# Hybrid decoder step on one core: the recurrence's input tiles moved one tile ahead of its gate tiles, and three steps of the sample attention moved by one or two half steps

## The chip, the cores and the metric

The kernel runs on one core of one Trainium2 chip. The metric is the device time of the whole program in microseconds (us). Engines are called as in the profile: PE is TensorE's matmul pipeline, PEld its weight loads, DVE VectorE, ACT ScalarE, POOL GpSimd, SP the engine that issues the DMAs. L1302 is line 1302 of the kernel. Lines from L105 on stand two or three higher in the changed kernel.

## The reference, cut to what matters

One layer of a decoder for a prompt of 512 tokens and a sample group of 8 x 8 tokens, which share the weights. One input projection feeds a sparse attention with three branches (compressed, selected, window) and a gated linear recurrence; both are merged and projected out.

```
z = einsum('btd,dc->btc', rms(x), w_in)       # one projection, 9776 columns
q, kv, g_nsa, g_att, x_rnn, g_rnn, gm_att, gm_rnn = split(z)
# recurrence, 1024 channels
xc = conv_b + sum(x_ext[:, k:k+T] * conv_w[k] for k in range(4))
r  = sigmoid(blockdiag(xc, w_rg) + b_rg)
i  = sigmoid(blockdiag(xc, w_ig) + b_ig)
log_a = -8 * r * softplus(-lru_lambda)
a, u  = exp(log_a), sqrt(-expm1(2*log_a)) * (i * xc)
h_t   = a_t * h_(t-1) + u_t
u_rnn = (h * silu(g_rnn)) @ w_rnn_out
# sample attention
o_cmp = softmax(q k_c) v_c                    # 64 compressed blocks
idx   = top_k(importance, 15)                 # from o_cmp's probabilities
o_sel = softmax(q k[idx], q k_new) v          # gathered blocks
o_win = softmax(q k_window) v_window          # last 512 tokens
```

## The kernel before, in words

All work is written out by hand in one order; every engine runs its own instructions strictly in that order and waits on semaphores. All weights are split into a high and a low part (`whi`, ACT, L233; `wlo`, DVE, L239), so that a product is three matmuls (L1798 to L1800). The projection is done in column tiles of 128; a tile is four **slots**, each with 24 of these matmuls of 288 columns. The main loop over slots emits, in this order: the high split of weights due, the sample attention's next half step if it is due, the low split, the evacuation of the sums of the slot before, the functions put behind this slot (`at(slot, fn, True)`), and then the slot's 24 matmuls.

`column_tiles()` sets the order of the tiles. The recurrence's channels come as eight chunks `c` of 128: tile `("rx", c)` holds its input, tile `("rg", c)` its gate path.

The sample's attention starts with these tiles. It runs over four **pairs** of sequences, one pair every six steps; a step is two **half steps** (0 and 1) and `put(t, half, order, f, x)` places a function. Half steps are spread evenly over the slots, so some slots have none. In half 0 stand `s_turn` (PE transposes of the exponentials into the two `t` banks, copied out by ACT as `spt`), `s_out` (values into banks `o` and `m`) and `k_scores` (into the two `s` banks, read by `k_max` on DVE and `s_exp` on ACT). A pair begins with `x_scores` (compressed scores, half 0, both `s` banks), read by `x_exp` (maximum on DVE, exponential on ACT, two additions on DVE); `x_sum` (one transposing product into a `t` bank, half 1 of the next step) feeds `x_select` on DVE, the choice of blocks. A pair ends with `x_turn_` (six transposes, both `t` banks), `x_turned` (five ACT copies to `vx`), `x_out` (products with `vx`), `s_sum` (DVE reads banks `o` and `m`), `s_fin` and `s_put`.

A chunk of the recurrence is a chain. When its `rx` tile is evacuated, `rnn_chunk(c, xr)` puts the convolution's first part on ACT (`xc`) and DVE; the rest of the convolution stands one slot later, `split` (high and low part of `xc`: `xb`, and of the block-diagonal weights: `bdh`, `bdl`) two slots later. From the third slot on `gate_0` is ready to be emitted, then `gate_1`: each is four matmuls (L1302) into one `s` and one `t` bank, and four ACT tanh that read them (`tr`, `ti`, L1305). A gate step is emitted only in a slot whose half step has none of `x_scores`, `k_scores`, `s_turn`, `x_turn_`, `c_norm`:

```
if gates and not taken:
    behind.setdefault(s, []).append(gates.pop(0))
```

One slot after `gate_1` follows `decay` (ACT exponential, tanh, square root; two DVE products), two slots after it `scan` (DVE; then two small ACT copies `hout`). `rnn_gated` multiplies by the gate path once both are there.

Slots are counted below from the one in which chunk 0's `rx` tile is evacuated (slot 0). In the trace of before, slot 4 begins near 736.2 us, slot 7 at 748.7, slot 13 at 778.9, slot 17 at 797.8, slot 28 at 859.4, slot 35 near 891.4.

Of the kernel before, what the change touches and what calls it, by code (L numbers as in the profile page):

```python
# [84 lines left out]
def column_tiles():  # L85

    off = dict(q=0, kv=1024, gn=2560, ga=2608, rx=3632, rg=4656, gma=5680, gmr=7728)

    def kv(br, s, g):
        return off["kv"] + ((br * 2 + s) * KG + g) * HD + np.arange(HD)  # L90

    tiles = [(("gn",), off["gn"] + np.arange(48))]
    fill = [(("ga", j), off["ga"] + j * 128 + np.arange(128)) for j in range(8)]
    fill += [(("gm", 1, j), off["gmr"] + j * 128 + np.arange(128)) for j in range(16)]
    fill += [(("gm", 0, j), off["gma"] + j * 128 + np.arange(128)) for j in range(16)]
    for g in range(KG):
        if g:
            tiles += [fill.pop(0) for _ in range(3)]
        tiles.append((("c", g), np.concatenate([kv(0, 0, g), kv(0, 1, g)])))
        tiles.append((("v", g), np.concatenate([kv(1, 1, g), kv(2, 1, g)])))  # L100
        tiles.append((("k", g), np.concatenate([kv(1, 0, g), kv(2, 0, g)])))
        for rp in range(2):
            tiles.append((("q", g, rp), off["q"] + (g * 4 + rp * 2) * HD + np.arange(128)))
    left = len(fill) - (EARLY - 9)
    tiles += fill[:-left]  # L105
    for c in range(8):
        tiles.append((("rx", c), off["rx"] + c * 128 + np.arange(128)))
        tiles.append((("rg", c), off["rg"] + c * 128 + np.arange(128)))
    tiles += fill[-left:]
    return tiles  # L110

# [2 lines left out]
def nsa_rglru_step(ctx, tc, a, o):  # L114
# [54 lines left out]
    tiles = []  # L169
# [21 lines left out]
    for n, (kind, m, units) in enumerate(tiles):  # L191
# [19 lines left out]
        for u in range(len(units)):  # L211
            late = len(units) == 1 or u == 0 and tiles[n - 1][0][0] == "G"
            at = base - 2 if late else base - 3 if u == 0 else base - 1
# [109 lines left out]
    for c in range(8):  # L323
        for b in range(2):
            k = 2 * c + b
            x = xs[c][:, b]
# [41 lines left out]
    def at(slot, fn, last=False):  # L368

        (behind if last else later).setdefault(slot, []).append(fn)  # L370

    now = [0]
# [302 lines left out]
    for g in range(KG):  # L675
        for i in range(4):
            for br in range(3):
                x = Group()
# [473 lines left out]
    def sample_steps():  # L1152

        steps = {}

        def put(t, half, order, f, *args):
            steps.setdefault(2 * t + half, []).append((order, len(steps.get(2 * t + half, [])), f, args))

        for x in pairs:
            s = 2 + 6 * x.n
            if x.b[0].b >= KEPT:
                for y in x.b:
                    put(s - 5, 1, 0, c_fetch, y)
            put(s - 2, 0, 9, q_pair, x)
            e = s - 3 if x.n else s - 2
            put(e, 0, 0, c_square, x)
            put(e, 1, 5, c_norm, x)
            put(e, 1, 7, c_root, x)  # L1170
            put(e + 1, 1, 7, c_keys, x)
            put(s, 0, 4, x_scores, x)
            put(s, 0, 8, x_exp, x)
            put(s, 1, 7, x_prob, x)
            put(s, 1, 9, x_new, x)
            put(s + 1, 1, 5, x_sum, x)
            put(s + 1, 1, 6, x_select, x)
            for k, n2 in enumerate((4, 0, 1, 2, 3)):
                t = s + 1 + k
                put(t - 1, 0, 0, k_load, x, n2)  # L1180
                put(t, 1, 0, v_load, x, n2)
                put(t, 0, 4, k_scores, x, n2)
                put(t, 0, 8, k_max, x, n2)
                put(t, 0, 9, s_exp, x, n2)
                put(t + 1, 0, 1, s_turn, x, n2)
                put(t + 1, 0, 1.5, s_turned, x, n2)
                put(t + 2, 0, 2, s_out, x, n2)
            put(s + 5, 1, 9, s_factors, x)
            put(s + 6, 1, 7, s_total, x)
            put(s + 6, 1, 1, x_turn_, x)  # L1190
            put(s + 6, 1, 1.5, x_turned, x)
            put(s + 7, 0, 4.5, x_out, x)
            put(s + 7, 1, 8, s_sum, x)
            put(s + 8, 1, 5, s_fin, x)
            put(s + 8, 1, 8, s_put, x)
        for t in range(max(steps) + 1):
            fs = [f for _, _, f, _ in steps.get(t, [])]
            taken.extend(f for f in fs if f in (x_scores, k_scores, s_turn, x_turn_, c_norm))
            for _, _, f, args in sorted(steps.get(t, []), key=lambda e: e[:2]):
                f(*args)  # L1200
            yield (t + 1) / (max(steps) + 1)
# [8 lines left out]
    gates, taken = [], []  # L1210

    def load_bd(c):
        t = rp_["p"].tile([128, 2, 128], F, tag="bd", name="bd", bufs=2)
        S.dma_start(t, a["w_bd"][c])
        bd[c] = t
# [42 lines left out]
    def rnn_chunk(c, xr):  # L1258
        p = rp_["p"]

        def rt(name):
            return p.tile([128, NT], F, tag="rt", name=name, bufs=5)

        if c + 1 < 8:
            load_bd(c + 1)
        xc = rt("xc")
        xs_ = xr[:, 515:603].rearrange("p (b s) -> p b s", s=11)
        V.tensor_copy(cvout[:, c, 0, :], xr[:, 512:515])
        V.tensor_copy(cvout[:, c, 1:, :], xs_[:, :, 8:11])
        xcs = xc[:, SEQ:].rearrange("p (b t) -> p b t", t=8)  # L1270
        A.activation(xc[:, :SEQ], xr[:, 0:SEQ], AF.Identity, bias=P("cb", c), scale=P("cw", c * 4))
        A.activation(xcs, xs_[:, :, 0:8], AF.Identity, bias=P("cb", c), scale=P("cw", c * 4))

        def tap(k):
            w = P("cw", c * 4 + k)
            V.scalar_tensor_tensor(xc[:, :SEQ], xr[:, k:k + SEQ], w, xc[:, :SEQ], OP.mult, OP.add)
            V.scalar_tensor_tensor(xcs, xs_[:, :, k:k + 8], w, xcs, OP.mult, OP.add)

        tap(1)
        at(now[0] + 1, lambda: (tap(2), tap(3)), True)  # L1280
        tr, ti, aa = rt("tr"), rt("ti"), rt("aa")

        xb = []

        def split():

            split_bd(c)
            for w in range(2):
                me, other = slice(w * 64, w * 64 + 64), slice(64 - w * 64, 128 - w * 64)
                t = p.tile([128, NT], R, tag=f"xb{w}", name="xb", bufs=1)  # L1290
                A.activation(t[me], xc[me], AF.Copy)
                V.tensor_sub(t[other], xc[me], t[me].bitcast(F))
                xb.append(t)

        def gate(w):

            me = slice(w * 64, w * 64 + 64)
            for h in range(2):
                hs = slice(h * HF, h * HF + HF)
                b = bank("st"[h])  # L1300
                for k in range(2):
                    T.matmul(b[:, :HF], bd[c][k][:, w, :], xb[w][:, hs], start=k == 0, stop=k == 1)  # L1302
                for n, t in enumerate((tr, ti)):
                    z = slice(n * 64, n * 64 + 64)
                    A.activation(t[me, hs], b[z, :HF], AF.Tanh, scale=0.5, bias=lc[z, 2 + w, c:c + 1])  # L1305

        def decay():
            A.activation(aa, tr, AF.Exp, scale=lc[:, 0, c:c + 1], bias=lc[:, 0, c:c + 1])
            A.activation(tr, tr, AF.Tanh, scale=lc[:, 1, c:c + 1], bias=lc[:, 1, c:c + 1])
            A.activation(tr, tr, AF.Sqrt, scale=0.25)  # L1310
            V.scalar_tensor_tensor(ti, ti, 1.0, xc, OP.add, OP.mult)
            V.scalar_tensor_tensor(ti, aa, 1.0, ti, OP.add, OP.mult)

        def scan():
            V.tensor_mul(ti, ti, tr)
            u0, a0 = ti[:, SEQ::8], aa[:, SEQ::8]
            V.tensor_mul(xc[:, 0:8], a0, sth[:, c])
            V.tensor_add(u0, u0, xc[:, 0:8])
            V.memset(a0, 0.0)
            hh = p.tile([128, NT], F, tag="hh", name="hh", bufs=1)  # L1320
            V.tensor_tensor_scan(hh, aa, ti, 0.0, OP.mult, OP.add)
            A.activation(hout[:, c, 0:1], hh[:, SEQ - 1:SEQ], AF.Copy)
            A.activation(hout[:, c, 1:], hh[:, SEQ + 7::8], AF.Copy)
            held["hh", c] = hh
            if ("s", c) in held:
                rnn_gated(c)

        at(now[0] + 2, split, True)

        def gate_0():  # L1330
            gate(0)
            gates.append(gate_1)

        def gate_1():
            gate(1)
            at(now[0] + 1, decay, True)
            at(now[0] + 2, scan, True)

        at(now[0] + 3, lambda: gates.append(gate_0))

    def rnn_gated(c):

# [310 lines left out]
    for s, (n, h, u) in enumerate(slots):  # L1653
# [98 lines left out]
        for n2 in range(n, len(tiles)):  # L1752
            if slot_of[n2] > s + 3:
                break
            name, j = tiles[n2][0][0], tiles[n2][0][-1]
            if name in ("ua", "ur") and s >= slot_of[last_g + 1] and (name == "ur", j) not in gates_in:
                t = gates_in[name == "ur", j] = rp_["p"].tile([128, NT], F, tag="tgi", name="tgi", bufs=4)
# [25 lines left out]
        for step, (h2, k) in enumerate([(h, k) for k in range(8)]):  # L1783
            kk = u * 8 + k
            name = kind[0]
# [115 lines left out]
```

## Time and profile before

| | |
|---|---|
| Time, median of 3 runs | 1646.51 us (1645.73 to 1646.8) |
| The profiled execution's own time | 1646.57 us |
| Its span, first to last instruction | 1644.5 us |
| PE busy | 1603.1 us, 97% of the span |
| DVE, ACT, POOL busy | 67%, 47%, 19% of the span |
| Mean granted TensorE clock | 0.992 of full speed |

Busy time of PE counts pipelined matmuls, so it says where PE stood still, not how fast it was while busy. The clock column says that: 1.0 is 2.4 GHz, 0.5 is 1.2 GHz.

### The profile page before, as it was taken

What the parts mean: (1) busy time and instruction counts of PE and PEld (TensorE: products, weight loads), DVE (VectorE), ACT (ScalarE), POOL (GpSimd) and SP (SyncE); (2) the same over time, 40 slices, a digit from 0 to 9 for tenths busy, and PEclk for the clock granted to TensorE, in tenths of its full rate; (3) what the DMA queues carried; (4) which work ended last, traced back from release to release, by engine and by line L of the source; (5) the groups of instructions that cost most, each with busy time, mean ns of one, the idle gap of its engine ahead of it and who ended that gap; (6) DMA issues with size and microseconds to landing.
All of it is one profiled execution on the core that took longest, in us unless ns stands there. A gap on an engine that the chain in (4) does not pass through costs nothing.

```text
span 1644.5 us, 34197 instructions
## 1 busy us (share of the span) xinstructions
PE 1603.1 (97%) x13293; PEld 1550.9 (94%) x13293; DVE 1104.0 (67%) x2159; ACT 775.9 (47%) x1429; POOL 305.7 (19%) x361
## 2 busy tenths in 40 slices
PE   9999999999999999999898999999999999999999
PEld 8989989998999999998788889999999999999999
DVE  7768778766876786666566575766666433458785
ACT  6353545454445554448666677444444222234332
POOL 0014443533443345400000000000000111110000
PEclk9999999999999999999999999999999999999999
DMA  6178534433443344448575674633328444466431
GB/s 231 63 273 273 187 106 130 161 114 107 157 140 112 116 147 157 146 140 256 180 227 192 218 236 142 202 140 126 126 107 300 157 163 147 143 219 218 150 136 70
DMA packets 131956, 271.91 MB, mean 165 GB/s; under 512 B 19793, under 2 KB 59858, under 8 KB 131538
## 3 DMA queue, kind: packets, MB, share of 16 engines
q1 hardware_dynamic: 131794, 269.73, 49.0%
q8 instruction: 104, 1.70, 0.4%
q14 instruction: 58, 0.48, 0.1%
HBM read 235.04 MB, written 43.02 MB: 169 GB/s over the span
## 4 chain that ended last, share of the span: by engine, by line
PE 47%; ACT 3%; DVE 3%; issue 0%; DMA 0%; POOL 0%; SPq 0%; ACTq 0%
PE g L1798 9%; PE g L1799 9%; PE g L1800 9%; PE g L1448 2%; PE g L1447 2%; PE g L1446 2%; PE g L1548 2%; PE g L1547 2%; PE g L1546 2%; PE t L1448 1%; PE t L1446 1%; PE t L1447 1%; PE s L941 1%; PE s L1548 1%; PE s L1546 1%; PE s L1547 1%
## 5 line engine op out<-in xcount | busy, mean ns | idle before, releaser
L1798 PE MATMUL g<-xh,whi 128*128 128x288 f32 x1920 | 580.8, 303 | 0.1
L1800 PE MATMUL g<-xh,wlo 128*128 128x288 f32 x1920 | 569.8, 297 | 3.7 <-DVE wlo L239 3.7
L1799 PE MATMUL g<-xl,whi 128*128 128x288 f32 x1920 | 570.1, 297 | 0.1
L1798 PEld LDWEIGHTS g<-xh,whi 128*128 128x128 f32 x1920 | 364.8, 190 | 17.0 <-issue 14.4
L1800 PEld LDWEIGHTS g<-xh,wlo 128*128 128x128 f32 x1920 | 364.2, 190 | 4.2 <-DVE wlo L239 4.2
L1799 PEld LDWEIGHTS g<-xl,whi 128*128 128x128 f32 x1920 | 364.7, 190 | 1.7 <-DVE xl L321 0.3
L239 DVE TENSOR_TENSOR wlo<-raw,whi 128x1024 fp32r<-128x1024 f32 x164 | 215.7, 1315 | 73.8 <-ACT whi L233 73.2
L879 POOL TENSOR_TENSOR cr<-cr,wcs 128x512 f32<-128x512 f32 x128 | 182.3, 1430 | 144.5 <-DMA cr<-in_cmp 140.4
L233 ACT ACTIVATE whi<-raw 128x1024 fp32r<-128x1024 f32 x164 | 172.5, 1052 | 30.4 <-PE g L1799 16.5
L746 ACT ACTIVATE p<-p,sm,rq 128x128 f32<-128x128 f32 (+3 forms) x128 | 82.9, 648 | 143.1 <-DVE sm L743 143.0
L765 DVE TENSOR_TENSOR pt<-t,pt 128x512 fp32r<-128x512 f32 x96 | 66.1, 689 | 69.9 <-ACT pt L764 68.8
L754 POOL TENSOR_SCALAR p<-p,sm 128x128 f32<-128x128 f32 (+3 forms) x128 | 69.5, 555 | 226.7 <-DVE sm L751 125.5
L589 POOL TENSOR_TENSOR ur<-ur,tgi 128x288 f32<-128x288 f32 x32 | 25.7, 805 | 400.6 <-DVE tgi L588 304.8
L764 ACT ACTIVATE pt<-t 128x512 fp32r<-128x512 f32 x96 | 56.6, 593 | 73.6 <-PE t L761 73.0
L885 DVE TENSOR_REDUCE skvx<-cr 128x16 f32<-128x512 f32 x128 | 86.7, 678 | 2.6 <-POOL cr L879 1.7
L595 ACT ACTIVATE mh<-ur 128x288 fp32r<-128x288 f32 x32 | 14.2, 444 | 143.6 <-POOL ur L589 143.6
L1800 PE MATMUL g<-hrh,wlo 128*128 128x288 f32 x256 | 75.6, 295 | 0.0
L1800 PE MATMUL g<-oah,wlo 128*128 128x288 f32 x256 | 75.6, 295 | 0.0
L1799 PE MATMUL g<-hrl,whi 128*128 128x288 f32 x256 | 75.5, 295 | 0.0
L1798 PE MATMUL g<-hrh,whi 128*128 128x288 f32 x256 | 75.5, 295 | 0.0
L1799 PE MATMUL g<-oal,whi 128*128 128x288 f32 x256 | 75.5, 295 | 0.0
L1798 PE MATMUL g<-oah,whi 128*128 128x288 f32 x256 | 75.4, 295 | 0.0
(440 smaller groups left out, 3599.4 us busy)
## 6 DMA issues: line engine op xcount, KB each, us to landing
raw<-in_w_in SPq DMA_DIRECT2D x124, 512.0 KB, 3.7
cr<-in_cmp SPq DMA_DIRECT2D x128, 256.0 KB, 3.6
kr<-in_selk SPq DMA_DIRECT2D x128, 128.0 KB, 3.3
vr<-in_selv SPq DMA_DIRECT2D x128, 128.0 KB, 2.9
a<-in_w_in SPq DMA_DIRECT2D x28, 512.0 KB, 4.2
tgi<-tg SPq DMA_DIRECT2D x32, 288.0 KB, 4.2
yr<-in_w_out SPq DMA_DIRECT2D x18, 512.0 KB, 5.1
raw<-in_w_rnn SPq DMA_DIRECT2D x16, 512.0 KB, 4.7
```

Source lines behind the costliest of these rows:

```text
L233: A.activation(hi, raw[k], AF.Copy)
L239: V.tensor_sub(lo, raw.pop(k), hi.bitcast(F))
L746: A.activation(p[:, :n], p[:, :n], AF.Exp, bias=sm[:, 1, r - r0:r - r0 + 1], scale=rq[:, i, r:r + 1], accum_out=sm[:, 2, r - r0:r - r0 + 1])
L754: G.tensor_scalar(p[:, :n], p[:, :n], sm[:, 3, r - r0:r - r0 + 1], 1.0, op0=OP.mult, op1=OP.mult)
L764: A.activation(hi, t, AF.Copy)
L765: V.tensor_sub(lo, t, hi.bitcast(F))
L879: G.tensor_tensor(v, v, wcs[:, :, None, :].to_broadcast([128, 4, 4, 32]), op=OP.mult)
L885: V.tensor_reduce(x.kvx[:, :, 8 + n * 4:12 + n * 4], v, axis=AX.X, op=OP.add)
L1446: T.matmul(gb[:, :HF], wh[:, i, :], r_h[:, HS[half]], start=begins and i == 0, stop=False, skip_group_check=True)
L1798: T.matmul(gb[:, :HF], wh[:, k, :], r_h[:, hs], start=kk == 0, stop=False)
L1799: T.matmul(gb[:, :HF], wh[:, k, :], r_l[:, hs], start=False, stop=False)
L1800: T.matmul(gb[:, :HF], wl[:, k, :], r_h[:, hs], start=False, stop=last and k == 7)
```

## The change

The tile order becomes rx0, rx1, rg0, rx2, rg1, ... rx7, rg6, rg7 (it was rx0, rg0, rx1, rg1, ...), so that chunks 1 to 7 are evacuated four slots earlier. `gate_0` becomes ready four slots after the evacuation instead of three. The tiles `tr`, `ti`, `aa` are taken when `gate_0` is emitted, no longer with the chunk. In the sample's attention `x_turn_` and `x_turned` move from half 1 of a pair's step 6 to half 0 of its step 7, `x_out` from step 7 to step 8, and `s_sum`, `s_fin`, `s_put` follow one step later. No instruction is added or removed.

```diff
-    for c in range(8):
-        tiles.append((("rx", c), off["rx"] + c * 128 + np.arange(128)))
-        tiles.append((("rg", c), off["rg"] + c * 128 + np.arange(128)))
+    for c in range(9):
+        if c < 8:
+            tiles.append((("rx", c), off["rx"] + c * 128 + np.arange(128)))
+        if c:
+            tiles.append((("rg", c - 1), off["rg"] + (c - 1) * 128 + np.arange(128)))
...
-            put(s + 6, 1, 1, x_turn_, x)
-            put(s + 6, 1, 1.5, x_turned, x)
-            put(s + 7, 0, 4.5, x_out, x)
-            put(s + 7, 1, 8, s_sum, x)
-            put(s + 8, 1, 5, s_fin, x)
-            put(s + 8, 1, 8, s_put, x)
+            put(s + 7, 0, 1, x_turn_, x)
+            put(s + 7, 0, 1.5, x_turned, x)
+            put(s + 8, 0, 3, x_out, x)
+            put(s + 8, 1, 8, s_sum, x)
+            put(s + 9, 1, 5, s_fin, x)
+            put(s + 9, 1, 8, s_put, x)
...
-        tr, ti, aa = rt("tr"), rt("ti"), rt("aa")
-        xb = []
+        xb, room = [], []
...
         def gate_0():
+            room.extend(rt(name) for name in ("tr", "ti", "aa"))
             gate(0)
             gates.append(gate_1)
...
-        at(now[0] + 3, lambda: gates.append(gate_0))
+        at(now[0] + 4, lambda: gates.append(gate_0))
```

What the move does to each engine's order is shown at three places. First ACT in slots 7 to 9. Before, after chunk 0's decay (`aa`, `tr`) stand the second chunk's evacuation and convolution (`xr`, `xc`), then chunk 0's `hout`:

```order
L1083 ACTIVATE spt<-t 128x512 x2
L1072 ACTIVATE sp,ssm<-sp,ssm 128x512 x2
L1308 ACTIVATE aa<-tr,lc 128x576
L1309 ACTIVATE tr<-tr,lc 128x576
L1310 ACT_TABLE_LOAD
L1310 ACTIVATE tr<-tr 128x576
L566 ACTIVATE xr<-g 128x224
L568 ACTIVATE xr<-g 128x8x8
L1271 ACTIVATE xc<-xr,par 128x512
L1272 ACTIVATE xc<-xr,par 128x64
L1322 ACTIVATE hout<-hh 128x1
L1323 ACTIVATE hout<-hh 128x8
```

Now the same piece of ACT's order, from the same decay on:

```order
L1310 ACTIVATE tr<-tr,lc 128x576
L1311 ACT_TABLE_LOAD
L1311 ACTIVATE tr<-tr 128x576
L578 ACT_TABLE_LOAD
L578 ACTIVATE rg<-g 128x288
L1324 ACTIVATE hout<-hh 128x1
L1325 ACTIVATE hout<-hh 128x8
L1305 ACTIVATE tr<-s,lc 64x288
L1305 ACTIVATE ti<-s,lc 64x288
L1305 ACTIVATE tr<-t,lc 64x288
L1305 ACTIVATE ti<-t,lc 64x288
L235 ACTIVATE whi<-raw 128x1024
```

The gate path's tanh (`rg`) stands where the convolution stood, and chunk 1's gate step is in slot 8, so its four tanh stand right behind chunk 0's `hout`; before, chunk 1's first gate step was in slot 12.

Second, PE around the first pair's end, slots 15 to 19 (the 24 matmuls of each slot are left out). Before, a light slot with `x_turn_` follows the next pair's `x_scores` (L941, 32x80):

```order
L1078 MATMUL t<-cst,sp 128x128 x8
L1095 MATMUL o<-vr,spt 32x64 x16
L1095 MATMUL m<-vr,spt 32x64 x16
L941 MATMUL s<-skvx,qb 32x80 x8
...
L1000 MATMUL t<-cst,se 80x128 x2
L1004 MATMUL t<-cst,skvx 80x128 x4
...
L1095 MATMUL o<-vr,spt 32x64 x16
L1095 MATMUL m<-vr,spt 32x64 x16
L941 MATMUL s<-kr,qb 32x512 x8
L1021 MATMUL o<-vx 32x64 x12
L1021 MATMUL m<-vx 32x64 x12
...
L969 MATMUL t<-se,cst 128x128
```

Now chunk 2's gate step (slot 16) follows `x_scores`, `x_turn_` (slot 17) stands in one slot with `s_out` and `k_scores`, and `x_sum` (L971) comes in the slot right behind it:

```order
L943 MATMUL s<-skvx,qb 32x80 x8
...
L1302 MATMUL s<-xb,bdh 128x288
L1302 MATMUL s<-xb,bdl 128x288
L1302 MATMUL t<-xb,bdh 128x288
L1302 MATMUL t<-xb,bdl 128x288
...
L1002 MATMUL t<-cst,se 80x128 x2
L1006 MATMUL t<-cst,skvx 80x128 x4
L1097 MATMUL o<-vr,spt 32x64 x16
L1097 MATMUL m<-vr,spt 32x64 x16
L943 MATMUL s<-kr,qb 32x512 x8
...
L971 MATMUL t<-se,cst 128x128
```

Third, ACT in slots 28 to 31, at the second pair's end, as it is now: `x_exp` (L959), chunk 4's convolution, chunk 3's decay, then `hout`, and only then the copies `vx` that free the `t` banks for `x_sum`:

```order
L959 ACTIVATE se,ssm<-s,ssm 128x64 x2
L568 ACTIVATE xr<-g 128x224
...
L1309 ACTIVATE aa<-tr,lc 128x576
L1310 ACTIVATE tr<-tr,lc 128x576
L1311 ACT_TABLE_LOAD
L1311 ACTIVATE tr<-tr 128x576
L235 ACTIVATE whi<-raw 128x1024
L996 ACT_TABLE_LOAD
L996 ACTIVATE se,ssm<-se,ssm 128x8 x4
L1324 ACTIVATE hout<-hh 128x1
L1325 ACTIVATE hout<-hh 128x8
L1013 ACTIVATE vx<-t,cst 80x256 x3
```

Before, this pair's `vx` followed `x_exp` directly, with no decay or `hout` between:

```order
L1083 ACTIVATE spt<-t 128x512 x2
L957 ACTIVATE se,ssm<-s,ssm 128x64 x2
L1011 ACTIVATE vx<-t,cst 80x256 x3
L1012 ACTIVATE vx<-t 80x256
L1013 ACTIVATE vx<-t 80x256
```

Counted so, `gate_0` of the eight chunks now stands 4, 4, 4, 5, 5, 4, 4 and 5 slots after its chunk's evacuation; before it stood 4, 4, 3, 4, 3, 5, 4 and 3 slots after it.

## Rows read from the trace of the kernel before

**Rows 1.** The page: span, and PE's busy time.

```profile
span 1644.5 us, 34197 instructions
PE 1603.1 (97%) x13293; PEld 1550.9 (94%) x13293; DVE 1104.0 (67%) x2159; ACT 775.9 (47%) x1429; POOL 305.7 (19%) x361
```

**Rows 2.** Waits of PE, 690 to 1040 us: total us, times, longest us.

```profile
PE s L1302 <- DVE xb L1292: 7.7, 3, 5.2
PE o L1021 <- ACT vx L1012: 4.7, 2, 2.9
PE t L1078 <- DVE ssq L926: 1.5, 1, 1.5
PE t L1000 <- ACT spt L1083: 1.4, 1, 1.4
PE s L1302 <- DVE ssm L1060: 1.1, 1, 1.1
PE t L1078 <- ACT ti L1305: 0.5, 1, 0.5
```

**Rows 3.** Stretches: length us, PE busy us (matmuls), granted clock, DMA share, GB/s.

```profile
750.64:757.11 6.47, 6.47 (x57) 1.00 0.80 256
808.34:812.58 4.24, 4.24 (x26) 0.75 0.86 272
896.78:903.20 6.42, 6.42 (x28) 0.54 0.00 0
932.81:935.11 2.30, 2.30 (x91) 1.00 0.00 0
```

**Rows 4.** PE in order of time: start us, length us, what.

```profile
736.51 0.37 PE L1302 MATMUL s<-xb,bdh 128*128 128x288 f32 x1
...
748.66 1.04 PE L1078 MATMUL t<-cst,sp 128*128 128x128 f32 x8
...
797.97 0.60 PE L1004 MATMUL t<-cst,skvx 128*80 128x128 f32 x4
```

**Rows 5.** ACT in order of time, slots 7 to 9 [idle before <- what ended it].

```profile
751.80 0.72 ACT L1072 ACTIVATE sp<-sp,ssm 128x512 f32<-128x512 f32 x1 [0.79 <-DVE ssm L1060]
...
755.01 1.28 ACT L1310 ACT_TABLE_LOAD   x1
756.30 0.69 ACT L1310 ACTIVATE tr<-tr 128x576 f32<-128x576 f32 x1
...
761.51 0.20 ACT L1322 ACTIVATE hout<-hh 128x1 f32<-128x1 f32 x1 [3.04 <-DVE hh L1321]
```

**Rows 6.** ACT, slots 33 to 36, where decay, split and scan of two chunks meet.

```profile
888.07 0.72 ACT L1072 ACTIVATE sp<-sp,ssm 128x512 f32<-128x512 f32 x1 [3.16 <-DVE ssm L1060]
...
899.91 0.20 ACT L1322 ACTIVATE hout<-hh 128x1 f32<-128x1 f32 x1 [3.36 <-DVE hh L1321]
```

**Rows 7.** ACT groups, 700 to 1040 us: busy us, mean ns of one | idle before.

```profile
L233 ACT ACTIVATE whi<-raw 128x1024 fp32r<-128x1024 f32 x36 | 37.9, 1053 | 10.3 <-PE g L1799 8.6 <-issue 1.2 <-ACT xr L566 0.2
L1305 ACT ACTIVATE ti<-t,lc 64x288 f32<-64x288 f32 x16 | 8.0, 497 | 0.3
```

**Rows 8.** DVE groups of the same stretch.

```profile
L239 DVE TENSOR_TENSOR wlo<-raw,whi 128x1024 fp32r<-128x1024 f32 x37 | 46.3, 1252 | 50.1 <-ACT whi L233 50.0
L1292 DVE TENSOR_TENSOR xb<-xc,xb 64x576 fp32r<-64x576 f32 x16 | 12.0, 753 | 0.8
L1321 DVE TENSOR_TENSOR_SCAN hh<-aa,ti 128x576 f32<-128x576 f32 x8 | 10.9, 1358 | 0.4
L577 DVE SCALAR_TENSOR_TENSOR rg<-rg,g 128x288 f32<-128x288 f32 x16 | 7.2, 453 | 14.5 <-ACT rg L576 14.4
L1315 DVE TENSOR_TENSOR ti<-ti,tr 128x576 f32<-128x576 f32 x8 | 6.0, 753 | 0.1
```

**Rows 9.** DVE's last read of `x_scores`' first bank; ACT's of `x_turn_`'s.

```profile
736.21 0.16 DVE L959 TENSOR_TENSOR se<-s,cst 128x8 f32<-128x8 f32 x1
...
806.27 0.37 ACT L1012 ACTIVATE vx<-t 80x256 f32<-80x256 f32 x1
```

More of the change, by code (lines that the diff above doesn't have):

```diff
@@ L1302, in gate @@
                     T.matmul(b[:, :HF], bd[c][k][:, w, :], xb[w][:, hs], start=k == 0, stop=k == 1)
-                for n, t in enumerate((tr, ti)):
+                for n, t in enumerate(room[:2]):
                     z = slice(n * 64, n * 64 + 64)
@@ L1307, in decay @@
         def decay():
+            tr, ti, aa = room
             A.activation(aa, tr, AF.Exp, scale=lc[:, 0, c:c + 1], bias=lc[:, 0, c:c + 1])
@@ L1314, in scan @@
         def scan():
+            tr, ti, aa = room
             V.tensor_mul(ti, ti, tr)
```

## Prediction

> **What bounds the kernel now.** I read the page first: PE is busy for 1603.1 of 1644.5 us [rows 1], so a change that adds and removes no instruction can only move the 41 us in which PE stands still, and the clock that goes with them. Next the waits of PE in the stretch that the change touches, 690 to 1040 us, all slots in which recurrence and sample attention run together: six groups, 16.9 us in sum [rows 2]. The reader is to see that two of them are the ones whose producers the change starts earlier: gate steps that wait for the low part `xb` (7.7 us in three waits) and `x_out` that waits for ACT's copies `vx` (4.7 us in two). Third, the clock in the stretches behind the two longest waits [rows 3]: 24 matmuls in 4.24 us at a mean of 0.75 after the 2.9 us wait, 28 in 6.42 us at 0.54 after the 5.2 us wait, where undisturbed 48 take 6.47 us at 1.00, 0.135 us each. The excess is 1.0 and 2.6 us; with the half-rate `x_out` ahead of the first I put it at 1.8, so waits of this size cost 4.4 us more than their length. Last, ACT and DVE in order of time around the waits, for what they do meanwhile.
>
> **What it removes.** Of the eight chunks, the three whose `gate_0` stood in the third slot after the evacuation are the three that waited for `xb`; the five in the fourth or fifth did not. Now all stand in the fourth or fifth, a slot of at least 3.24 us later: the 7.7 us go, but for a rest of the 5.2 us wait, which I put at nothing since the new order takes other work out of that chunk's way. `x_out` now has a light slot more, so the 4.7 us go. The other 4.5 us belong to slots whose neighbours change; I drop them too and price what replaces them below. With the clock's 4.4 us: span 1644.5 - 16.9 - 4.4 = 1623.2 us, if nothing new came.
>
> **What it adds.** Gates and transposes only have two `s` and two `t` banks each, shared with scores and `s_turn`. A bank comes free when ACT or DVE has read it, and both engines work in order. So I look for slots where a bank's reader now stands behind something late.
>
> *A, slots 6 to 9.* Chunk 1's `gate_0` is in slot 8, with chunk 0's scan, and its tanh stand on ACT behind `hout`, which waits for that scan (first order piece). `s_turn` of slot 9 needs that `t` bank for its second half. PE gets there, counted from the end of slot 7's `k_scores`: two slots' matmuls 6.5 [rows 3], the gate's four 0.5, half an `s_turn` 0.5 [rows 4]: 7.5 us. ACT, counted from the same point (750.64): the exponential starts 1.16 later, the square root ends 5.19 after that [rows 5]. From there to `hout` before took 4.5 us, with a convolution in between; now there stand a table load 1.28 [rows 5], the gate path's tanh 0.5 and product 0.45, the product 0.75 and the scan 1.36 with three small operations 0.4 [rows 7, 8]: 4.7. `hout` 0.25, four tanh 2.0 [rows 7]. Sum 13.3 us, so PE waits 5.8 us. On the way there ACT has chunk 1's convolution and split ahead of slot 6's tanh, which delays `k_max` and through it slot 6's gate (about 1.1 us) and, by those tanh, slot 7's `s_turn` (about 1.5); of that delay some 0.7 is left in slot 7. A = 1.1 + 1.5 + 6.5 = 9.1 us, between 5.8 and 12.
>
> Here the Trainium skill can be weighed. The loads take 1.28 us in the trace, and the square root starts 0.01 us behind one [rows 5]. The Trainium skill, ScalarE: Activation LUTs, "What ACT_TABLE_LOAD costs", adds a drain to each and gives about 2.66 us per switch. By the Trainium skill the chain with its two loads would be 2.8 us longer and A 11.9. The row shows no drain, and I go by the row.
>
> *B, slot 16.* Chunk 2's `gate_0` follows `x_scores` and needs the `s` bank that `x_exp` still reads (second order piece). Where ACT is not behind, this costs nothing: in slot 4 DVE's last read ended at 736.37 and the gate went at 736.51 [rows 4, 9]. But now slots 13 and 14 hold chunk 1's decay and scan with chunk 2's convolution and split, as slots 33 and 34 did before for chunks 3 and 4; there, from the exponential to `hout`, it took 11.84 us [rows 6]. From the end of slot 13's `k_scores`: `k_max` 0.8, that 11.84, `hout` 0.25, `whi` 1.05, `wlo` 1.15 [rows 7, 8], then the maximum, exponential and two additions 0.9: 16.0 us. PE is there after three slots' matmuls 9.7 and `s_turn`, `s_out`, `x_scores` 2.3 [rows 3]: 12.0. B = 4.0 us, between 0 and 6.
>
> *C, slots 31 and 32.* `x_sum` needs a `t` bank that `x_turn_` filled one slot before; before it had two. In the first pair ACT's last read of it ended at 806.64, 8.7 us after the second half of the transposes began at 797.97 [rows 4, 9], because `hout` and its scan stood ahead of `vx`. PE now wants the bank 5.9 us after that point (rest of `x_turn_` 0.6, `s_out` and `k_scores` 2.1 by their neighbours, matmuls 3.24): a wait of 2.8 us. With the change this concerns the second pair, where decay and scan now stand ahead of `vx` (third piece); in the first pair they no longer do, and there PE has just stood still in B. Behind `vx` ACT has the window's exponentials, the split and `whi`, and DVE the products `xb` twice 0.75 and `wlo` 1.25 [rows 8] ahead of `x_select`, which frees the bank for `s_turn` of slot 32: about 6.9 us, where PE is there after 3.9; another 3.0. C = 5.8 us, between 0 and 8.
>
> *D, the rest.* `s_sum` now ends one half step before the next pair's first `s_out` overwrites its banks (two had been), `s_fin` shares both `t` banks with `c_norm`, and the gate in slot 40 stands behind a scan by one slot. Each can cost 0 to 2 us; such small waits were 4.5 us before [rows 2]. I take 3, between 1 and 6. POOL's clearing of the one `xr` buffer now waits for the convolution of a chunk four slots earlier only at chunk 1, 0.8 us with nothing behind it; weight loads on SP keep their slots.
>
> *Clock.* A's wait is of the size of the 5.2 us one (2.6), B's and C's of the 2.9 us one (1.8 each): 6.2 us, between 2 and 9.
>
> **The sum.** 1623.2 + 9.1 + 4.0 + 5.8 + 3 + 6.2 = 1651.3 us of span. The profiled execution took 2.1 us more than its span, and its 1646.57 us is the median of the runs within 0.1 us: 1653.4 us, call it 1653. The change would take 21 us of waits and clock away and put 28 in their place.
>
> **The rivals.** *Faster.* The new waits happen only where PE comes early; once PE has stood still in A, ACT and DVE have caught up, and B and C may find their banks free. Then 1623.2 + 9.1 + 2.6 + 1 + 2.1 = 1638 us; without A too, some 1629. For it speaks slot 4, where `x_exp` kept up; against it that B's chain runs from `k_scores` of its own slot, whatever lead there was, and that the same chain took 11.84 us once before. It decides at B: if ACT reaches `hout` within 8 us of the exponential, it holds.
>
> *No change.* A stands and one of B and C: 1638 + 4.0 + 1.8 = 1644 or 1638 + 5.8 + 1.8 = 1646 us.
>
> *Slower by more.* If each of A to D is at its upper end: 1623.2 + 12 + 6 + 8 + 6 + 9 + 2.1 = 1666 us.
>
> *The table's drain.* If each switch of ACT's tables took a drain beside the load, A and B would each grow, in the direction of my forecast. The row has 0.01 us between load and use, so I give it 3 in 100, within the cases above 1649.8. By the Trainium skill's rule weighed above it would be 1653 + 2.8 = 1656 us at least.
>
> **How the numbers follow.** My forecast with its range of 1650 to 1661 has a chance of 0.56, still slower than that 0.05, no change 0.22, faster 0.17. The bounds of A to D reach from 1638 to 1666; I leave out what lies above 1661 and the case without A below 1638, together under 2 in 10. A measurement of this kernel tells 0.2% (3.3 us) from no change: faster is below 1643.2, slower above 1649.8. That gives 0.17, 0.22 and 0.61.
>
> **What would show it.** In the new profile, waits of L1302 for `xb` and of `x_out` for `vx` should be gone. In slot 9 a wait of `s_turn` for ACT's `ti`, 5 to 8 us long, with a half clock behind it, shows A. A gate's wait for `se` or the reader of the `s` bank in slot 16 shows B, `x_sum` waiting for `vx` C. The forecast is wrong if PE's waits in the stretch sum to less than 17 us. That ACT takes less time between exponential and `hout` than in the rows, or that PE reaches slot 9 later, would do it.

## The result, and the profile after

The changed kernel takes 1654.94 us (median of 5 runs, 1652.91 to 1657.49), the kernel before 1646.47 us (median of 5 beside them): a ratio of 1.0052, with a 95% interval of 1.0038 to 1.0067. It is slower by some 8.5 us; 1653 was forecast.

The page of the changed kernel, with the lines that answer to [rows 1]:

```profile
span 1653.2 us, 34205 instructions
PE 1606.9 (97%) x13293; PEld 1551.4 (94%) x13293; DVE 1107.2 (67%) x2159; ACT 778.9 (47%) x1431; POOL 303.7 (18%) x361
```

PE has the same 13293 matmuls and 3.8 us more of busy time; it stands still for 46.3 us where it was 41.4. Half-speed stretches, which make the same matmuls longer, hold some 2.5 of the 3.8: behind the long waits the clock gives away 7.1 us (worked out below), before it was 4.6 (a mean of 0.76 in the 7 us from 806.69, 0.58 in the 7 us from 896.78). ACT has two instructions more, and both are table loads (24 in 690 to 1060 us, 22 before): the program is given no new instruction, but its new order needs two more loads.

The waits of PE in the stretch of the change, 690 to 1060 us, against [rows 2]:

```profile
PE t L1080 <- ACT ti L1305: 9.9, 4, 6.0
PE s L1302 <- DVE ssm L958: 4.1, 1, 4.1
PE t L971 <- ACT vx L1014: 2.3, 1, 2.3
PE s L1302 <- DVE ssm L1062: 1.6, 1, 1.6
PE m L1097 <- DVE to L1126: 1.1, 1, 1.1
PE t L1080 <- DVE ssq L928: 0.9, 1, 0.9
PE t L1080 <- ACT spt L1085: 0.7, 1, 0.7
...
```

The reader is to see that the rows on which the change works are gone: no gate waits for `xb` (7.7 us before), `x_out` doesn't wait for `vx` (4.7 before). In their place stand 21.3 us of others, where 16.9 were. In order of time, PE again, the waits of over 1 us but the last, each in brackets behind its matmul:

```profile
751.26 0.66 PE L1080 MATMUL t<-cst,sp 128*128 128x128 f32 x4 [1.48 <-ACT ti L1305]
766.45 1.11 PE L1080 MATMUL t<-cst,sp 128*128 128x128 f32 x4 [6.00 <-ACT ti L1305]
808.25 0.58 PE L1302 MATMUL s<-xb,bdh 128*128 128x288 f32 x1 [4.06 <-DVE ssm L958]
887.50 0.49 PE L971 MATMUL t<-se,cst 128*128 128x128 f32 x2 [2.32 <-ACT vx L1014]
935.05 0.37 PE L1302 MATMUL s<-xb,bdh 128*128 128x288 f32 x1 [1.56 <-DVE ssm L1062]
940.93 0.66 PE L1080 MATMUL t<-cst,sp 128*128 128x128 f32 x4 [1.50 <-ACT ti L1305]
```

They are `s_turn` of slots 7 and 9 (A), the gate of slot 16 (B), `x_sum` of slot 31 (C), and the gate of slot 40 with the `s_turn` behind it (part of D).

The wait of slot 9 read backwards, first on ACT, then on DVE, both in order of time:

```profile
759.59 1.28 ACT L578 ACT_TABLE_LOAD   x1
...
764.18 0.20 ACT L1324 ACTIVATE hout<-hh 128x1 f32<-128x1 f32 x1 [2.88 <-DVE hh L1323]
...
765.90 0.50 ACT L1305 ACTIVATE ti<-t,lc 64x288 f32<-64x288 f32 x1
```

```profile
761.33 0.45 DVE L579 SCALAR_TENSOR_TENSOR rg<-rg,g 128x288 f32<-128x288 f32 x1 [3.86 <-ACT rg L578]
761.70 0.75 DVE L1317 TENSOR_TENSOR ti<-ti,tr 128x576 f32<-128x576 f32 x1
...
762.78 1.36 DVE L1323 TENSOR_TENSOR_SCAN hh<-aa,ti 128x576 f32<-128x576 f32 x1
```

PE starts at 766.45, 0.05 us after the fourth tanh has ended. Ahead of the tanh stands `hout` (ACT idle for 2.88), ahead of `hout` the scan, ahead of the scan on DVE the gate path's product, and this waited 3.86 us for a tanh that stands behind a table load. Slot 16 hangs on the same chain a chunk later. ACT, from the exponential that begins it to `hout`, and DVE behind it:

```profile
792.80 0.72 ACT L1074 ACTIVATE sp<-sp,ssm 128x512 f32<-128x512 f32 x1 [1.73 <-DVE ssm L1062]
...
804.74 0.20 ACT L1324 ACTIVATE hout<-hh 128x1 f32<-128x1 f32 x1 [3.35 <-DVE hh L1323]
```

```profile
806.03 1.23 DVE L241 TENSOR_TENSOR wlo<-raw,whi 128x1024 fp32r<-128x1024 f32 x1 [1.32 <-ACT whi L235]
...
808.01 0.22 DVE L958 TENSOR_REDUCE ssm<-s 128x1 f32<-128x64 f32 x1
```

From exponential to `hout` 11.94 us, where the forecast took 11.84 from [rows 6]. Behind `hout` stands `whi` on ACT, for which DVE's `wlo` waits, and behind `wlo` the maximum of `x_exp` that PE waits for.

The clock behind the three long waits, 7 us each (columns as in [rows 3]):

```profile
766.45:773.45 7.00, 7.00 (x97) 4.84 (x98) 2.73 (x6) 3.80 (x8) 0.00 (x0) 0.58 0.50 156
808.25:815.25 7.00, 7.00 (x50) 6.80 (x54) 2.36 (x16) 4.83 (x16) 1.78 (x6) 0.64 0.75 226
887.50:894.50 7.00, 6.31 (x38) 5.91 (x42) 5.35 (x14) 5.36 (x11) 0.00 (x0) 0.76 0.84 260
```

A mean of 0.58 is mostly the lower of the two levels, 1.2 GHz; 7 us at 0.58, 0.64 and 0.76 give away 2.9, 2.5 and 1.7 us, 7.1 in sum.

### The profile page after: what moved, and what is told of

It reads as the page before. It is cut to its first block, busy times and chain, and to the rows that moved or that the text cites. A ratio compares the mean times of both kernels' runs of the same rounds, so it can differ in the third digit from the quotient of the medians.

```text
span 1653.2 us, 34205 instructions
## 1 busy us (share of the span) xinstructions
PE 1606.9 (97%) x13293; PEld 1551.4 (94%) x13293; DVE 1107.2 (67%) x2159; ACT 778.9 (47%) x1431; POOL 303.7 (18%) x361
## 4 chain that ended last, share of the span: by engine, by line
PE 72%; DVE 13%; ACT 9%; issue 2%; DMA 2%; SPq 1%; POOL 0%; ACTq 0%; POOLq 0%; DVEq 0%
PE g L1801 15%; PE g L1803 15%; PE g L1802 15%; DVE wlo L241 3%; ACT whi L235 2%; PE g L1449 2%; PE g L1450 2%; PE g L1451 2%; PE t L763 2%; ACT p L748 1%; DVE p L744 1%; PE g L1549 1%; PE g L1550 1%; PE g L1551 1%; DVE pt L767 1%
## 5 line engine op out<-in xcount | busy, mean ns | idle before, releaser
L241 DVE TENSOR_TENSOR wlo<-raw,whi 128x1024 fp32r<-128x1024 f32 x164 | 220.0, 1341 | 83.7 <-ACT whi L235 79.0
```

The lines of the kernel that those rows point to most:

```text
L241: V.tensor_sub(lo, raw.pop(k), hi.bitcast(F))
```

## The experiments

The theory to test: the old waits go as the change is made to do, but readers of the shared `s` and `t` banks now stand on ACT and DVE behind the chain decay, table loads, gate path, scan, `hout` of a chunk, and PE waits for them at A, B and C, with the clock on top. The rivals are in the expectations. Times stand beside 1646.2 to 1647.5 us of the kernel before in the same sessions; the changed kernel's own time is 1654.94.

### One half of the change at a time

**e1_tiles**: the changed kernel with the sample steps where they were.

```diff
-            put(s + 7, 0, 1, x_turn_, x)
...
-            put(s + 8, 0, 3, x_out, x)
...
+            put(s + 6, 1, 1, x_turn_, x)
...
+            put(s + 7, 0, 4.5, x_out, x)
...
```

> This kernel makes the tile half of the change alone: rx tiles one ahead, gate_0 four slots behind, rt tiles taken late; the sample steps stay where they were before. Theory (a bank's reader stands behind late work): the 7.7 us of xb waits go with about 3 us of clock; A stays as in the changed kernel, because gate_0 of chunk 1 is still in slot 8 behind scan 0 (7.5 us of waits, 3 of clock); B and C are absent, since no gate stands in slot 16 and x_sum has its bank two half steps later; the vx waits of before (4.7 us) stay. 1646.5 - 10.7 + 10.5 = about 1646 us, between 1643 and 1650. Rival 1 (the longer chain itself loads ACT and DVE): it holds the whole loss, 1653 to 1656 us. Rival 2 (the sample moves alone are the loss): it keeps the gain of the xb waits, 1636 to 1640 us.

**e2_puts**: the kernel before with the sample steps of the change, the same lines the other way round.

> This kernel makes the sample half of the change alone: x_turn_, x_out and what follows a half step later; tiles and gates by the rules of before, except that gates of chunks 2 to 4 stand in other slots (20, 22, 27, 29, 37, 38), since the slots that keep them out have moved. Theory: the vx waits go (4.7 us and 2 of clock), A and B are absent (chunk 1's gates stand in 12 and 14, none in 16), xb waits stay where a gate is in the third slot; C may show since x_sum has half a step less. 1646.5 - 6.7 + 0 to 5 = 1640 to 1646 us. Rival 1 (the longer chain is the loss): 1636 to 1642. Rival 2 (the sample moves are the loss): 1653 to 1656 us.

Measured: 1660.73 us (ratio 1.0079, 1.0067 to 1.0091) and 1660.52 us (1.0082, 1.0069 to 1.0095). Both expectations failed, and both times lie above every range given: each half alone is slower than the two together. PE in order of time, the tile half first, then the sample half:

```profile
768.08 1.12 PE L1080 MATMUL t<-cst,sp 128*128 128x128 f32 x4 [5.99 <-ACT ti L1305]
849.07 1.09 PE L1080 MATMUL t<-cst,sp 128*128 128x128 f32 x4 [3.20 <-DVE ssq L928]
922.77 0.63 PE L1080 MATMUL t<-cst,sp 128*128 128x128 f32 x4 [2.90 <-DVE ssq L928]
977.05 0.64 PE L1132 MATMUL t<-cst,t 128*64 128x128 f32 x2 [4.29 <-ACT spt L1085]
```

```profile
858.55 0.58 PE L1302 MATMUL s<-xb,bdh 128*128 128x288 f32 x1 [8.91 <-DVE xb L1292]
957.41 0.49 PE L969 MATMUL t<-se,cst 128*128 128x128 f32 x2 [4.09 <-ACT vx L1012]
```

Of the tile half, A stands as expected (5.99), B and C are absent and the `xb` waits are gone. But the gates now stand in other slots (chunk 2's in 19 and 21), and with them came three waits of 2.9 to 4.3 us that I had not seen, for `c_norm`'s bank and in `s_fin`. One more thing differs from what was expected: the `vx` waits were to stay here, and they are gone. In the sample half chunk 3's gate moved into the third slot after its evacuation (slot 27) and waits 8.9 us for `xb`, and `x_sum` waits for `vx` (6.5 us in two waits) where `x_out` did. So it is the tile order that takes the `vx` waits away, and not the later `x_out`. The two halves are not two sums that add up: each moves the slots that keep gates out, and with them all the later gates.

### The bank or the chain

**e4_tt**: chunk 2's first gate takes two banks of `t`.

```diff
-                b = bank("st"[h])
+                b = bank("tt"[h] if (c, w) == (2, 0) else "st"[h])
```

> This is the changed kernel with one edit: chunk 2's gate_0 in slot 16 takes both its banks from the pair t, not one from s and one from t, so that it does not wait for the bank that x_exp reads. Theory (B: the wait is for that bank alone): the 4.1 us wait of slot 16 goes with about 2.5 us of clock; x_turn_ in slot 17 now waits for the tanh on both t banks and gives up to 2 us back: 1655 - 6.6 + 1 = about 1649 us, between 1647 and 1651. Rival 1 (ACT is behind by 4 us there and any bank will show it): x_turn_ or k_scores of slot 17 wait instead, 1653 to 1656 us.

**e5_sum_s**: the third pair's `x_sum` takes a bank of `s` (and `x_select` reads it there).

```diff
-        x.m = bank("t")
+        x.m = bank("s" if x.n == 2 else "t")
```

> This is the changed kernel with one edit: the third pair's x_sum (slot 31) takes a bank of the pair s and not of t, so that it does not wait for vx, the copies that ACT makes of x_turn_'s banks. Theory (C: the copies stand behind decay, scan and hout of chunk 3, and the t banks come free late): the 2.3 us wait of x_sum goes with about 1.7 us of clock; x_select is earlier, but s_turn of slot 32 needs the same t banks half a slot later and keeps its 0.7 us or grows to at most 1.5: 1655 - 3.5 = about 1651 us, between 1649 and 1653. Rival 1 (ACT is late by that much whatever the bank, as chunk 2's gate on two t banks showed for slot 16): k_scores or s_turn of slot 32 wait 2 us instead, 1654 to 1656 us.

Measured: 1656.05 us (1.0052, 1.004 to 1.0065) and 1654.06 us (1.005, 1.0036 to 1.0064), both as the changed kernel within what can be told. PE, two rows of the first, one of the second:

```profile
805.25 0.40 PE L1302 MATMUL t<-xb,bdh 128*128 128x288 f32 x1 [2.38 <-ACT spt L1085]
811.99 0.41 PE L1002 MATMUL t<-cst,se 128*80 128x128 f32 x2 [1.01 <-ACT ti L1305]
```

```profile
886.74 0.77 PE L971 MATMUL s<-se,cst 128*128 128x128 f32 x2 [3.29 <-DVE ssm L1067]
```

Slot 16's 4.06 us became 2.38 for another late reader, 1.01 in slot 17 and 0.4 behind that: 3.8 in sum. Slot 31's 2.32, and slot 32's 0.69 with it, became 3.29. The rival holds in both places: the reader of the other bank is late as well, and the bank only decides which one PE meets.

### Moving the gates

**e3_gate10**: chunk 1's first gate not in slot 8, behind scan 0, but in slot 10, beside `c_norm`.

```diff
-                if gates and not taken:
+                if gates and any(f.__name__ == "scan" for f in behind.get(s, [])):
+                    put_off.append(s)
+                elif gates and not [f for f in taken if not (put_off and f is c_norm)]:
                     behind.setdefault(s, []).append(gates.pop(0))
+                    put_off.clear()
```

> This is the changed kernel with one edit: chunk 1's gate_0 is not put into the slot that holds scan 0 (slot 8) but into slot 10; every other gate stands as it did. Theory (A: in slot 8 the gate's tanh stand behind scan 0 and hout, and s_turn of slot 9 needs the t bank they read): the 6.0 us wait of slot 9 goes, with about 3 us of clock; the 1.5 us wait of slot 7 stays: 1655 - 9 = 1646 us, between 1644 and 1648. Rival 1 (ACT is behind in this stretch whatever the bank): the wait comes back in slots 11 to 13 with its clock, 1652 to 1656 us. Rival 3 (PE's stop in slot 9 is what lets ACT catch up, so that B grows without it): B's wait in slot 16 grows from 4.1 to 6 us or more, 1648 to 1651 us.

**e8_skip16**: chunk 2's gates in slots 18 and 20, not in 16 and 18.

```diff
-                if gates and not taken:
+                if gates and not taken and s != skip[0]:
...
+            skip[0] = now[0] + 4 if c == 1 else -1
             at(now[0] + 1, decay, True)
```

> This is the changed kernel with one edit: chunk 2's gates stand in slots 18 and 20, not in 16 and 18. Theory (B: ACT and DVE are about 4 us late in slot 16, and any reader there waits; two slots later they are not): the 4.1 us wait goes with 2.5 us of clock, x_turn_ of slot 17 has 3.2 us of matmuls in between and waits under 1 us: 1655 - 6 = 1649 us, between 1648 and 1651. Rival 1 (the lateness has no end in these slots): x_turn_ or x_sum wait 3 us or more in slots 17 and 18, 1653 to 1656 us.

Measured: 1651.74 us (1.0026, 1.0017 to 1.0034), 3.2 us better than the changed kernel, where 9 were expected (by the ratios to the kernel before, 1.0026 for 1.0052, it is some 4); and 1658.46 us (1.0065, 1.0051 to 1.0079), 3.5 us worse, where 6 better were expected. In the first, slot 9 has no wait any more, so the step is right as to the place; but 0.8 us came back in slot 10, and 2.46 in slot 11. ACT, then PE:

```profile
770.01 1.28 ACT L929 ACT_TABLE_LOAD   x1
...
772.02 1.28 ACT L1305 ACT_TABLE_LOAD   x1
...
774.85 0.50 ACT L1305 ACTIVATE ti<-t,lc 64x288 f32<-64x288 f32 x1
```

```profile
775.40 0.66 PE L1080 MATMUL t<-cst,sp 128*128 128x128 f32 x4 [2.46 <-ACT ti L1305]
```

Beside `c_norm` the gate's tanh stand behind two other table loads, those of its square root. In the second kernel B's wait is gone, with two of 1.1 us in slot 18; but chunk 2's decay and scan went with the gates into slots 21 and 22, and slot 24, where 0.88 and 0.54 us were waited, now has a long one (PE), with ACT idle for 3.35 us at `hout` ahead of it:

```profile
851.66 0.66 PE L1080 MATMUL t<-cst,sp 128*128 128x128 f32 x2 [5.21 <-DVE ssq L928]
```

### Shortening the chain

**e6_hout_dve**: DVE makes the two copies into `hout`.

```diff
-            A.activation(hout[:, c, 0:1], hh[:, SEQ - 1:SEQ], AF.Copy)
-            A.activation(hout[:, c, 1:], hh[:, SEQ + 7::8], AF.Copy)
+            V.tensor_copy(hout[:, c, 0:1], hh[:, SEQ - 1:SEQ])
+            V.tensor_copy(hout[:, c, 1:], hh[:, SEQ + 7::8])
```

> This is the changed kernel with one edit: the two small copies into hout, which ACT makes behind each scan, are made by DVE. Theory (ACT, which works in order, stands still for the scan at hout, 3.35 us in slot 14 of the changed kernel, and with it all that a bank waits for): the wait of slot 9 falls from 6.0 to about 4.3 us (the tanh still wait for the buffer that the scan's addition frees, 1.4 us ahead of the scan's end), that of slot 16 from 4.1 to about 3.0 (DVE's wlo no longer waits for whi), that of slot 31 by up to 1; with the clock 4 to 6 us: 1649 to 1651 us. Rival 1 (DVE's chain is what is late, and ACT would wait for it in any case): the waits fall by less than 1 us together, 1653 to 1656 us.

**e7_hout_scan**: the same, and the scan in the slot of its decay.

```diff
-            at(now[0] + 2, scan, True)
+            at(now[0] + 1, scan, True)
```

> This is the changed kernel with two edits: hout by DVE, and scan put behind decay in the same slot, not in the next. Theory (what is late is the chain decay, table loads, SiLU tanh, scan, and the readers behind it): the scan no longer waits for the second table load and the tanh of the gate path, and ends 3 us or more earlier; the wait of slot 9 falls from 6.0 to 2 to 3.5 us, that of slot 16 from 4.1 to 1 to 2, that of slot 31 to under 1; k_max in the slot of the decay is not delayed, since it stands ahead. With the clock 8 to 13 us: 1642 to 1647 us, at or below the kernel before. Rival 1 (DVE is short of time and only shifts the lateness): new waits for k_max or xb of 3 us and more in the slots behind the decay, 1650 to 1656 us.

**e9_no_loads**: a copy in place of the chunk's square root.

```diff
-            A.activation(tr, tr, AF.Sqrt, scale=0.25)
+            A.activation(tr, tr, AF.Copy, scale=0.25)
```

> This is the changed kernel with the square root of each chunk's decay left out: a scaled copy of the same size stands in its place, so that the values are not the reference's, and the two table loads around it, 1.28 us each in the rows, 16 in all, are gone. Theory (A, B and C are the length of the chain decay, loads, gate path, scan): every wait behind that chain shortens by the two loads, 2.6 us: slot 9 from 6.0 to 3.4, slot 16 from 4.1 to 1.5, slot 31 from 2.3 to under 1; slot 7 keeps its 1.5. With 3 to 5 us of clock: 1655 - 11 = about 1644 us, between 1642 and 1647. Rival (the loads are covered by other waits of ACT): slot 9 and slot 16 fall by less than 1 us each, 1651 to 1655 us. The Trainium skill, ScalarE: Activation LUTs, "What ACT_TABLE_LOAD costs", gives about 2.66 us for a switch with its drain: by it slot 9's wait would fall by 5.3 us, to under 1, and slot 16's to nothing, 1638 to 1641 us.

Measured: 1651.42 us (1.0026, 1.0017 to 1.0036); 1654.73 us (1.0045, 1.0031 to 1.0059); 1645.42 us (0.9998, 0.9988 to 1.0007). The waits of the first and of the third kernel, 690 to 1060 us:

```profile
PE t L1080 <- ACT ti L1305: 8.4, 4, 4.2
PE t L1080 <- ACT spt L1085: 3.7, 1, 3.7
PE s L1302 <- DVE ssm L958: 2.9, 1, 2.9
PE t L1006 <- ACT ti L1305: 1.7, 1, 1.7
...
PE t L971 <- ACT vx L1014: 0.8, 1, 0.8
```

```profile
PE t L1080 <- ACT ti L1305: 7.2, 4, 3.3
PE s L1302 <- DVE ssm L958: 2.0, 1, 2.0
...
PE t L971 <- ACT vx L1014: 1.0, 1, 1.0
```

This shows the chain: shorten it, and all three waits shrink. With `hout` on DVE, A falls from 6.0 to 4.2, B from 4.1 to 2.9, C from 2.3 to 0.8, near what was expected, and the time by 3.5 us. Part comes back: `s_turn` of slot 32 waits 3.7 us for `spt` where it was 0.7, `x_turn_` of slot 17 waits 1.7. Without the loads A falls by 2.72, B by 2.05, C by 1.3, and the time by 9.5 us, within the expected range (slot 32's wait grows to 1.9). The Trainium skill, ScalarE: Activation LUTs, "What ACT_TABLE_LOAD costs", gives about 2.66 us for a switch with its drain; by it A would fall by some 5.3 us, an estimate for two switches. The trace doesn't bear out a drain beside the load: 2.72 were measured, against 2.56 for two loads of 1.28.

The earlier scan brought A down to 2.79 us and B to 2.57, but put the scan ahead of DVE's work for others, and the time is 3.3 us above that with `hout` alone. The first of these waits is the gate of slot 40, 1.6 us in the changed kernel; the others are for `x_sum`, `s_turn` and `s_out`, and new or larger:

```profile
PE s L1302 <- DVE ssm L1062: 3.2, 1, 3.2
...
PE t L971 <- DVE ssm L1068: 2.5, 1, 2.5
PE t L1080 <- DVE imp L978: 2.4, 1, 2.4
PE o L1097 <- issue: 2.0, 1, 2.0
```

The rival holds for this edit: DVE only passes the lateness on.

### Towards a better version

**e10_hout_ts**: `hout` on DVE, and each gate takes its `t` bank first.

```diff
-                b = bank("st"[h])
+                b = bank("ts"[h])
```

> This is the changed kernel with hout copied by DVE, as before in the run of that edit alone (1651.4 us), and a gate's first half in a bank of t, its second in one of s, where it was the other way. Theory (s_turn needs the t bank first in the next slot, and ACT's two tanh of 0.5 us each for the bank of s stand between): each wait of s_turn for a gate's tanh falls by 1.0 us: slot 7 from 1.5 to 0.5, slot 9 from 4.2 to 3.2, slot 28 from 0.9 to 0, slot 41 from 1.8 to 0.8, and x_turn_ of slot 17 from 1.7 to 0.7; k_scores, which needs the s banks, comes over 1 us later in its slot and does not wait: 1651.4 - 5 = 1646 to 1648 us, about the kernel before. Rival 1 (the lateness only moves on): k_scores wait for the tanh 1 us in four or five slots, 1650 to 1653 us.

**e11_before_hout**: the kernel before with `hout` on DVE and nothing of the change.

> This is the kernel before with hout copied by DVE and no part of the change. Theory (ACT stands still for the scan at hout; in the kernel before 3.05 us ahead of the copies vx): the 2.9 us wait of x_out for vx goes, the second of 1.8 us shrinks, the xb waits stay since they stand behind the table loads and not behind hout: 1646.7 - 4 to 6 = 1641 to 1643 us. Rival 1 (a wait taken away comes back a slot or two later on the same chain): 1645 to 1648 us. If the theory holds for both kernels, the edit is worth as much here as in the changed one (3.5 us), and the change is no better with it.

Measured: 1647.39 us (1.0008, 0.9998 to 1.0018), so the two edits give back all that the change cost, but win nothing over the kernel before; and 1648.75 us (1.0015, 1.0006 to 1.0024). In the first, the waits of `s_turn` in slots 7 and 28 and of `x_turn_` in slot 17 are gone, and `k_scores` waits once, for 1.1 us. Slot 9's 4.18 fell by less than the 1.0 us expected (PE):

```profile
765.72 0.66 PE L1080 MATMUL t<-cst,sp 128*128 128x128 f32 x4 [3.55 <-ACT ti L1305]
```

The second missed its forecast: the edit that won 3.5 us in the changed kernel costs some 2.5 us here, where 4 to 6 were to be won, and the time lies above the rival's range too. The 2.9 us wait for `vx` is gone, as expected, but the other grew from 1.8 to 2.8, and the wait of the next gate from 2.05 to (PE):

```profile
816.17 0.58 PE L1302 MATMUL s<-xb,bdh 128*128 128x288 f32 x1 [5.96 <-DVE xb L1292]
```

No version that was run is measurably faster than the kernel before; neither is the one without the square root, which computes something else.

### The clock by itself

**e12_fill**: matmuls added where PE would stand still, the computation unchanged.

```diff
+    def fill(t, n):
+        for _ in range(n):
+            T.matmul(t, xh[0][:, :128], xh[0][:, :HF], start=True, stop=True)
...
         s_scores([t[:, :80] for t in x.x], x, lambda n, c: x.b[n].kvx[:, c, :])
+        if x.n == 1:
+            fill(x.x[1][:, 128:416], 27)
...
         for u in UNITS:
+            if (x.n, n2, u) == (0, 0, 1):
+                fill(bank("s")[:, :HF], 40)
```

> This is the changed kernel with matmuls of 288 columns added that compute nothing which is used: 40 (5.4 us at 0.135) between the halves of slot 9's s_turn, where PE waits 6.0 us, and 27 (3.6 us) behind slot 15's x_scores, ahead of the 4.1 us wait of slot 16. The chains on ACT and DVE are as late as before, so nothing is gained but the clock. Theory (the fall of the granted clock to half speed behind the two waits is PE's standing still, and cost 3.0 and 2.5 us by the rows): the waits shrink to about 0.6 us each, the stretches behind them run at a mean clock of 1.00, and the time falls by 5.5: 1655 - 5.5 = about 1649.5 us, between 1648 and 1651.5. Rival (the clock falls there for a reason that has nothing to do with the waits, or the added work moves the fall to another place): 1653 to 1657 us.

Measured: 1651.63 us (1.0036, 1.0022 to 1.005), 3.3 us less than the changed kernel with 67 matmuls more, and just above the expected range. With five runs each this is near the limit of what the times can tell (the ratios' intervals, 1.0022 to 1.0050 and 1.0038 to 1.0067, overlap), so the trace has to decide. Windows behind the two places:

```profile
769.07:776.07 7.00, 7.00 (x114) 5.85 (x115) 3.06 (x7) 5.32 (x10) 0.00 (x0) 1.00 0.42 142
808.24:815.24 7.00, 5.33 (x78) 4.87 (x82) 2.35 (x16) 4.83 (x16) 2.38 (x10) 1.00 0.65 199
```

The clock is at its full level in both, where it was 0.58 and 0.64, and the waits left are 0.72 and 0.52 us. From slot 7's wait to that of slot 47 it takes 217.52 us (753.88 to 971.40), before the edit 220.71 (751.26 to 971.97): 3.2 us less. `x_turn_` of slot 17, which PE now reaches earlier, waits 1.67 us; so the clock gave back some 4.9 us of the 5.5 that the rows say, and that wait on the chain took a third of it.

## Why the prediction was right

The total is right, 1651.3 us of span against 1653.2, and its sum of new waits too: 21.9 us forecast, 21.3 measured. The terms inside it are not all of their size, and one has the wrong reason. With the measured waits and clock in their places the sum gives 1623.2 + 21.3 + 7.1 = 1651.6 us; the 1.6 us that are left stand in no row of a wait.

- **What goes.** All of the `xb` and `vx` waits named went. For `xb` the reason holds as far as it was tried: they are gone in e1_tiles, and in e2_puts the 8.9 us stand at a gate in the third slot. For `vx` it does not: the step put it on the light slot that `x_out` now has, but e1_tiles, without that slot, has no wait for `vx`, and e2_puts, with it, has 6.5 us of them at `x_sum`: the tile order did it. In the kernel before, ACT stood idle for 3.05 us at a `hout` shortly ahead of the first pair's `vx` (804.04, 805.20); in e1_tiles the `hout` of that stretch is long done (805.95, 812.52). Of the other rows of [rows 2], which the step dropped, the wait for `ssq` stays in slot 24, 0.88 us for 1.47.
- **A, 9.1 forecast, 7.5 measured.** Slot 7's 1.5 measured 1.48, slot 9's 6.5 measured 6.00, its chain `hout` and four tanh behind the scan, as the step said. The 1.1 us for slot 6's gate is absent.
- **B, 4.0 forecast, 4.06 measured**, on a chain of 11.94 us against 11.84. The step put it as the wait for the bank that `x_exp` reads; by e4_tt the chain is the cause, and a `t` bank shows it too (3.8 us in sum).
- **C, 5.8 forecast, 3.0 measured**: 2.32 for `x_sum` (2.8) and 0.69 in slot 32 (3.0). The second part had the wrong reader and was mis-sized: the wait there was for `spt`, not for `x_select`, and short. In e6_hout_dve, where PE is not held up as long in slot 31, it is 3.7 us, again for `spt`.
- **D, 3 forecast, 6.7 measured**, all the other waits, from slot 24 on. Three were named: slot 40's gate behind a scan (1.56), slot 47's `s_out` behind `s_sum` (1.10), and slot 24's, for the banks of `c_norm` and `s_fin` (0.88 and 0.54). The `s_turn` behind slot 40's gate (1.50) and slot 28's (0.94) were not. The most mis-sized term is here, 3.7 us too small; that A and C are 4.4 us too large together, so that the sum comes out, is luck.
- **Clock, 6.2 forecast, 7.1 measured**; for A and B e12_fill shows that it follows PE's standing still, for C this was not tried.
- **The rivals.** The faster case rested on ACT catching up while PE stands in A. B waits 4.06 us behind the 6.00 us of A, and 4.08 in e3_gate10, where slot 9 has no wait and slots 10 and 11 have 3.3 us: B does not depend on A and hangs on its own slots' chain, as the argument against that rival said.

What the forecast did not have is that these waits are not independent. In e4_tt, e5_sum_s, e8_skip16 and e11_before_hout a wait taken away came back, nearly whole or larger, within eight slots, in e3_gate10 about half of it, and the sums of waits in the stretch lie between 14 and 26 us for all kernels that were run. Whether some order of gates keeps all of them clear of the chain is open; it wasn't found here.

## What to carry to other kernels

When a step is moved to be rid of a wait, price the in-order queues that it now stands in, not the wait: the reader that sits behind a late chain is what PE meets next, through whichever buffer. A chain that two engines hand to and fro (ACT and DVE are busy here for only 236.4 and 224.6 of the 370 us from 690 to 1060) is shortened by taking work out of it, such as a copy that waits or a table load. Moving what waits for it is a gamble: of the five such moves that were run, a later gate (e3_gate10) and another order of the two banks (e10_hout_ts) won 3 to 4 us, another bank won nothing twice, and a later gate (e8_skip16) cost 3.5. Nor does an edit that pays in one order have to pay in another: `hout` on DVE won 3.5 us in the changed kernel and lost some 2.5 in the kernel before. Trace each half of a change that moves slots by itself before adding up their prices.

## What was unexpected of the hardware

Added matmuls that compute nothing made the stretch that they stand in 3.2 us shorter: with PE kept at work through the two waits, the 7 us behind them ran at a granted clock of 1.00 and not 0.58 and 0.64. And ACT's table loads cost in the chain little more than their rows say, 1.28 us each: without two of them a wait behind them fell by 2.72 us.
